# A transformer block on one Trainium2 core: weights between block products and heads split sooner, the second sums of x on GpSimd, the gates of the first head one product sooner

## The chip, the cores and the metric

One core of a Trainium2 chip runs the whole kernel in one launch. The metric is the time of one execution on the device in microseconds; the kernel before took 791.63 us (median of 3 runs, 791.51 to 792.37).

Names in the profile: PE is TensorE (PEld its weight loads), DVE is VectorE, ACT is ScalarE, POOL is GpSimd, SP is SyncE, which issues most of the DMAs. L93 is line 93 of the kernel that the profile belongs to. All line numbers in the text up to the prediction are those of the kernel before.

## The reference

A block with 512 tokens and a model width of 1024: a norm, one wide input projection, a gated linear attention (GLA) with 4 heads in two directions, a latent attention (MLA) with 8 heads, a merge of the two by gates, an output projection, and an MLP with a squared ReLU. Cut to what matters here:

```python
proj = rmsnorm(h, g_mix) @ w_in
(gq, gk, gv, gr, z_gf, z_gb, cq, ckv, kr, z_ma, z_mb) = split(proj)
# GLA, for each of 4 heads, forward and backward, in chunks:
la = log_sigmoid(z_g @ w_gate + b_gate) / 16
b = cumsum(la)                       # the decays
scores = (q * exp(b)) @ (k * exp(-b)).T, masked
y_gla = rmsnorm(scores @ v + state part) * silu(gr)
# MLA from the latents cq (384 wide) and ckv (256 wide), with rotary parts
merged = sigmoid(z_ma) * y_gla + sigmoid(z_mb) * y_mla
h = h + merged @ w_out
h = h + square(relu(rmsnorm(h) @ w_ff1)) @ w_ff2
return rmsnorm(h, g_final)
```

Everything is float32 and has to be computed to nearly that precision.

## The kernel before

**Three matmuls for one.** A float32 operand is split into a high part that TensorE takes as it is (`fp32r`) and the rest, the low part. A product is then high x high, high x low and low x high (`mm3`, L88 to L90). `split` (L92) makes the two: ScalarE copies the high half (L93), VectorE subtracts it from the source (L94). A product can't start before the high half of its weights is there, nor go beyond its second matmul before the low half is.

**Weights.** `weights` (L218) takes a staging tile `wf` (3 buffers), loads it by a DMA from SP's queue, takes tiles for the halves (`wh`, `wl`, 4 buffers each) and splits. `proj_begin` (L231) does that for 128 columns of `w_in` and takes a PSUM bank; `proj_run` (L235) issues the 24 matmuls of 128x512. A 512 KB load waits until its staging buffer's last reader is done, so the loads run about three projections ahead.

**The order of work.** Instructions are traced in the order of the Python code. A scheduler then sets each engine's order, except where `in_program_order` chains the instructions of an engine as they were traced, and `goes_behind` puts one stretch behind another. Each engine then works through its own queue in order; an instruction that waits holds up all behind it.

**The stretch that is edited** runs from the projections' beginning to the end of the GLA heads:

1. `x_sums` (L533): from the transposed input `xraw`, GpSimd makes sums `xy` (two per pair of blocks, L541 and L542), which are split into `xsy`. `more_x_sums` (L551) makes the sums `xz` on VectorE (L556, L557) and splits them into `xsz`.
2. Two block products, `gr` and `gv` (class `Seven`, L563), each a 512x1024x1024 product done as a Strassen-like scheme of seven half-size products, in the order 1, 2, 5, 6, 3, 7, 4. `prepare(m)` subtracts blocks of weights in place on VectorE (L580) and splits them; `product(m)` runs 24 matmuls of 128x512 onto two PSUM banks and evicts: products 1, 5 and 6 by a ScalarE copy (L627), products 2, 3 and 7 by a VectorE addition in place (L632) and then a sink, product 4 by the sink alone. Products 1, 6, 7 and 4 add onto the same two banks (`grx`, `gvx`), products 5 and 3 onto two others (`grz`, `gvz`). The sink of `gr` (`gr_rows`) is a tanh and a product (L640, L641), that of `gv` (`gv_rows`) a scaled split (L97, L98).
3. Between these products stand other projections, the `fillers`: `zb4` behind product 2 of `gr`, `z_chunk` (the weights `wz`, for gates and rotary keys) behind its product 7, `gq1` behind product 2 of `gv`. A loop (from L934) prepares two products ahead.
4. `gates_begin(h)`: two matmuls of the gates of head h, abs, exp and log on ScalarE (L413 to L418), a minimum on VectorE (L415). `gates_end(h)`: for each direction (`decays`) four scans on VectorE (L431), a difference (L435), three exponentials on ScalarE (L439, L440, L446), small copies on GpSimd. `gla_qk`: four products on VectorE (L460) and scaled copies on GpSimd (L468).
5. The heads loop: scores of head h, gates of head h+1, projections `za`, `gq`, `gk`, the product with v (`gla_out`), the row squares, the gated rows (L689), and `gla_turn`, which transposes them (`y`, L699). In the last round `ckv0`, `ckv1` and `cq0` (class `Latent`) stand where `gq` and `gk` stood.

From `heads_from` to the loop's end ScalarE and VectorE keep the traced order (`SPLITTERS`); TensorE keeps it from the first block product on (`PE_ONLY`); GpSimd keeps it in the stretch of 1 to 3.

Of the kernel before, what the change touches and what calls it, by code (L numbers as in the profile page):

```python
# [14 lines left out]
AF = mybir.ActivationFunctionType  # L15
# [41 lines left out]
def tile_block(ctx: ExitStack, tc: tile.TileContext, t, out: bass.AP):  # L57
# [13 lines left out]
    def u4(name, dt=F32R, shape=(P, 2, S)):  # L71
        return tl(list(shape), dt, "u4", 26, name)
# [4 lines left out]
    def ps(tag, name):  # L77
        serial[0] += 1
        return pp.tile([P, S], F32, tag=tag, bufs=4, name=f"{name}_{serial[0]}")
# [27 lines left out]
    def traced():  # L107
        return len(nc.cur_bb.bb.instructions)
# [15 lines left out]
    def goes_behind(late, early, engines):  # L124

        ins = nc.cur_bb.bb.instructions
        for e in engines:
            a, b = [[i for i in ins[x:y] if i.engine == e] for x, y in (early, late)]
            if a and b:
                issued_after(b[0], a[-1].name)  # L130
# [98 lines left out]
    def proj_begin(w, col, name, tag="mm"):  # L229
        wh, wl = weights(w[:, col : col + P], name)  # L230
        return wh, wl, ps(tag, name)  # L231

    def proj_run(begun, src, half=None, ks=range(KD)):
        wh, wl, acc = begun
        c = slice(0, S) if half is None else slice(half * 256, half * 256 + 256)  # L235
        for k in ks:
            mm3(acc[:, c], wh[:, k, :], wl[:, k, :], src[k][:, 0, c], src[k][:, 1, c], k == 0, k == KD - 1)
        return acc
# [106 lines left out]
    def gated(acc, name):  # L345

        z = u2(f"z{name}")
        nc.vector.tensor_tensor(z, acc, R, op=ALU.mult)
        th = u2(f"t{name}")
        nc.scalar.activation(th, z, AF.Tanh, scale=0.5)  # L350
        return z, th

    def qk_normed(h, x, acc):
        n = u2(f"{'gq' if x == 0 else 'gk'}n{h}")
        if x == 0:
            nc.vector.scalar_tensor_tensor(n, acc, GQ_SCALE, R, op0=ALU.mult, op1=ALU.mult)
        else:
            nc.vector.tensor_tensor(n, acc, R, op=ALU.mult)
        return n
# [15 lines left out]
                gates[d][64:128, :], wg_raw[d][64:128, :], raw(gates[d][64:128, :]), op=ALU.subtract  # L375
            )

    def z_chunk(tag):
        wf = stage(KD, 64, "wz")
        w3 = w_in.rearrange("(k p) w -> p k w", p=P)  # L380
        nc.sync.dma_start(wf[:, :, 0:32], w3[:, :, C_ZG : C_ZG + 32])
        nc.sync.dma_start(wf[:, :, 32:64], w3[:, :, C_KR : C_KR + 32])

        w, _ = halves(KD, P, "wz")
        split(w[:, :, 0:64], w[:, :, 64:128], wf)
        acc = ps(tag, "zk")
        for k in range(KD):
            for x in range(2):
                nc.tensor.matmul(
                    acc, w[:, k, :], xT[k][:, x, :], start=k == 0 and x == 0, stop=k == KD - 1 and x == 1  # L390
                )
        both = u2("zkl")
        nc.scalar.activation(both[0:64, :], acc[64:128, :], AF.Copy)
        nc.vector.tensor_tensor(both[0:64, :], acc[0:64, :], both[0:64, :], op=ALU.add)
        nc.vector.tensor_tensor(kr[0:64, :], both[0:64, :], R[0:64, :], op=ALU.mult)
        nc.scalar.activation(z4[0:32, :], kr[0:32, :], AF.Copy)
        nc.vector.tensor_tensor(z4[32:64, :], kr[0:32, :], raw(z4[0:32, :]), op=ALU.subtract)
        nc.vector.tensor_copy(z4[64:128, :], raw(z4[0:64, :]))
        for a, b in ((32, 48), (48, 32)):
            nc.sync.dma_start(kswap[a + 32 : a + 48, :], kr[b : b + HALF, :])  # L400
            nc.sync.dma_start(kr[a + 32 : a + 48, :], kr[a : a + HALF, :])
# [19 lines left out]
    def gates_end(begun):  # L421
        l, ms = begun
        return {d: decays(d, l[:, i], ms[i]) for i, d in enumerate(("f", "b"))}
# [25 lines left out]
    def project_qk(h, x):  # L449
        col, name = ((C_GQ, "gq"), (C_GK, "gk"))[x]  # L450
        qk[h, x] = qk_normed(h, x, proj_T(col + h * P, f"{name}{h}"))
# [81 lines left out]
    def x_sums():  # L533

        add = nc.gpsimd.tensor_tensor
        for p in range(KD // 2):
# [10 lines left out]
            x_left.append({m: (src[:, 0, c], src[:, 1, c]) for m, src, c in (  # L547
                (1, upper, LO), (2, lower, LO), (4, lower, HI), (5, sy, LO), (6, sy, HI),
            )})

    def more_x_sums():  # L551
        add = nc.vector.tensor_tensor
        for p in range(KD // 2):
            a, b = xraw[p], xraw[p + KD // 2]
            z = u2(f"xz{p}")
            add(z[:, LO], a[:, LO], a[:, HI], op=ALU.subtract)  # L556
            add(z[:, HI], b[:, LO], x_y[p][:, HI], op=ALU.subtract)  # L557
            sz = u4(f"xsz{p}")
            split(sz[:, 0], sz[:, 1], z)
            x_left[p][7] = sz[:, 0, LO], sz[:, 1, LO]  # L560
            x_left[p][3] = sz[:, 0, HI], sz[:, 1, HI]
# [147 lines left out]
    class Latent:  # L709
        def __init__(self, col, n, gcol, name):  # L710
            self.col, self.n, self.gcol, self.name = col, n, gcol, name
            self.cs, self.sqs = [], []

        def begin(self, j):
            self.begun = proj_begin(w_in, self.col + j * P, f"{self.name}{j}")

        def run(self, j):
            acc = proj_run(self.begun, xT)
            c = u2(f"{self.name}c{j}")
            nc.scalar.activation(c, acc, AF.Copy, scale=gvec[:, self.gcol + j : self.gcol + j + 1])  # L720
            s = u2(f"{self.name}s{j}")
            nc.scalar.activation(s, acc, AF.Square)
            if self.sqs:
                nc.vector.tensor_tensor(s, s, self.sqs[-1], op=ALU.add)
            self.cs.append(c)
            self.sqs.append(s)
# [187 lines left out]
    def zb_gate(f, tag="mm"):  # L914
        g2.append(gated(proj_T(C_ZB + f * P, f"zb{f}", tag), f"b{f}")[1])
# [7 lines left out]
    for x in (0, 2, 1, 3):  # L923
        sevens[0].load(x)
    loading = loading, traced()
    fillers = {
        (0, 2): lambda: zb_gate(4), (0, 7): lambda: z_chunk("mm"),
        (1, 2): lambda: project_qk(1, 0),
    }
    steps = [(a, m) for a in range(2) for m in SEVEN]  # L930
    ordered = traced()
    for a, m in steps[:2]:
        sevens[a].prepare(m)
    for n, (a, m) in enumerate(steps[:-2]):  # L934
        ahead = steps[n + 2]
        filled = (a, m) in fillers
        if a == 0:
            for x in {3: (0,), 7: (2, 1), 4: (3,)}.get(m, ()):
                sevens[1].load(x)
        if filled:  # L940
            sevens[a].product(m)
            at = traced()
            fillers[a, m]()
            goes_behind((at, traced()), loading, (mybir.EngineType.SP,))
        sevens[ahead[0]].prepare(ahead[1])
        if n == 2:
            more_x_sums()
        if (a, m) == (0, 5):
            load_gates()
            pos_i = u2("pos_i", I32)  # L950
            nc.gpsimd.dma_start(pos_i, t["positions"][0].partition_broadcast(P))
        if (a, m) == (0, 4):
            split_gates()
        if not filled:
            sevens[a].product(m)
# [1 line left out]

    def begin(col, name):  # L960
        return proj_begin(w_in, col, name)

    def begin_za(f):
        return begin(C_ZA + f * P, f"za{f}")

    def begin_qk(h, x):
        col, name = ((C_GQ, "gq"), (C_GK, "gk"))[x]
        return begin(col + h * P, f"{name}{h}")

    heads_from = traced()  # L970
    gated_now = gates_begin(0)
    w_k = begin_qk(1, 1)
    parts = gates_end(gated_now)
    sevens[1].product(7)
    near, nxt, far = gla_qk(0, parts)
    w_b = begin(C_ZB + 5 * P, "zb5")
    qk[1, 1] = qk_normed(1, 1, proj_run(w_k, xT))
    sevens[1].product(4)
    w_a = begin_za(0)
    g2.append(gated(proj_run(w_b, xT), "b5")[1])  # L980
    ckv_, cq_ = Latent(C_CKV, 2, V_KV, "ckv"), Latent(C_CQ, 3, V_Q, "cq")
    for h in range(GH - 1):
        sc = gla_scores(near, nxt, far)
        gated_now = gates_begin(h + 1)
        w_b = begin_za(2 * h + 1)
        acc = proj_run(w_a, xT)
        parts = gates_end(gated_now)
        za_gate(2 * h, acc)
        os = gla_out(h, sc)
        near, nxt, far = gla_qk(h + 1, parts)  # L990
        if h < 2:
            w_a = begin_qk(h + 2, 0)
        else:
            ckv_.begin(0)
        rs = gla_squares(h, os)
        za_gate(2 * h + 1, proj_run(w_b, xT))
        if h < 2:
            w_b = begin_qk(h + 2, 1)
            gla_gated(h, os, rs)
            qk[h + 2, 0] = qk_normed(h + 2, 0, proj_run(w_a, xT))  # L1000
            w_a = begin_za(2 * h + 2)
            qk[h + 2, 1] = qk_normed(h + 2, 1, proj_run(w_b, xT))
        else:
            ckv_.run(0)
            ckv_.begin(1)
            gla_gated(h, os, rs)
            ckv_.run(1)
            cq_.begin(0)
        gla_turn(h)
    in_program_order(heads_from, SPLITTERS)  # L1010
    in_program_order(ordered, PE_ONLY)
# [411 lines left out]
```

## Time and profile before

| what | value |
|---|---|
| median of 3 runs | 791.63 us |
| the profiled execution, whole | 793.04 us |
| its span, first to last instruction | 791.3 us |
| TensorE busy | 765.2 us, 97% |
| VectorE busy | 572.5 us, 72% |
| ScalarE busy | 442.7 us, 56% |
| GpSimd busy | 107.5 us, 14% |
| block product `gr` on TensorE, with its fillers | from 40.62 to 91.27 us |
| block product `gv`, with its fillers and the first gates | from 91.27 to 146.87 us |
| first scores of head 0 | 153.40 us |
| `cq0`, last projection of the heads loop | from 264.64 us |

The profile comes from one execution. Matmuls are pipelined and their ends are modelled, so 97% says that TensorE rarely waits, not that it works at its peak. A busy share is a mean over the whole span; a single stretch has its own limit.

In a timeline a line reads: start in us from the span's start, duration, engine, line, operation, tile written <- tiles read, partitions x elements, count, and in brackets how long the engine was idle before and which instruction ended it. In the list of waits a line reads: engine, tile and line that waited, then what it waited for, and us in total, times, longest.

### The profile page before, as it was taken

Reading aid. Unit: us, or ns where it says so; the run is one execution under the profiler, and the core shown is the slowest. Engines: PE = TensorE matmul, PEld = TensorE weight load, DVE = VectorE, ACT = ScalarE, POOL = GpSimd, SP = SyncE. Lnnn points to the kernel's source line nnn. Section 1 sums busy time; section 2 is a strip of 40 time slices with the busy share of each in tenths; the row PEclk is TensorE's granted clock in tenths of the full one; section 3 lists DMA queues with packets and bytes.
Section 4 is the critical chain, followed back from the end, with each engine's and each line's share of the span. In section 5 each row is a group of like instructions: output and inputs, shape, how many; then the busy total and the mean of one; then the engine's idle time right before and its main releaser. Section 6 shows DMA issues by size and latency. Waiting matters only on the chain.

```text
span 791.3 us, 10153 instructions
## 1 busy us (share of the span) xinstructions
PE 765.2 (97%) x3768; PEld 641.6 (81%) x3768; DVE 572.5 (72%) x858; ACT 442.7 (56%) x749; POOL 107.5 (14%) x182
## 2 busy tenths in 40 slices
PE   9999998899998999999999999999999999999996
PEld 7777876778786788888988898888888888888885
DVE  7799986665556667599993478875788487857695
ACT  7556547473745455698872366544653456436644
POOL 0400000442606002321120000000000000000014
PEclk9999999999999999999999999999999999999999
DMA  9617111212212433322114642064105501450002
GB/s 324 221 43 222 35 27 27 55 28 80 54 53 57 133 48 75 90 75 60 54 41 152 215 153 70 16 208 138 48 27 180 166 27 53 157 169 23 27 1 106
DMA packets 93185, 73.94 MB, mean 93 GB/s; under 512 B 15088, under 2 KB 74480, under 8 KB 93136
## 3 DMA queue, kind: packets, MB, share of 16 engines
q1 hardware_dynamic: 92048, 70.14, 30.1%
q10 hardware_dynamic: 864, 2.38, 0.8%
q0 software_dynamic: 224, 0.79, 0.4%
q8 instruction: 29, 0.48, 0.3%
q14 instruction: 20, 0.16, 0.1%
HBM read 69.62 MB, written 2.10 MB: 91 GB/s over the span
## 4 chain that ended last, share of the span: by engine, by line
PE 79%; DVE 11%; ACT 8%; issue 2%; POOL 1%; DMA 0%; SPq 0%; POOLq 0%; DVEq 0%; ACTq 0%
PE f L89 7%; PE f L90 7%; PE f L88 7%; PE gx L88 4%; PE gx L89 4%; PE gx L90 4%; PE first L311 2%; PE wo L88 2%; PE wo L89 2%; PE gz L89 2%; PE wo L90 2%; PE gz L90 2%; PE gz L88 2%; PE tp L891 2%; PE zb L90 1%
## 5 line engine op out<-in xcount | busy, mean ns | idle before, releaser
L1362 POOL DMA_DIRECT2D gfin<-in_g_final x1 | 0.7, 653 | 282.6 <-PE f L90 282.6
L1187 DVE TENSOR_TENSOR w<-w,w 128x1024 f32<-128x1024 f32 x32 | 38.7, 1220 | 0.4
L874 DVE TENSOR_REDUCE top<-s 128x1 f32<-128x512 f32 x32 | 21.7, 679 | 5.2 <-PE s L90 5.1
L877 ACT ACTIVATE e<-s,top 128x512 f32<-128x512 f32 x32 | 21.9, 686 | 5.6 <-DVE top L874 2.9
L1134 DVE TENSOR_TENSOR h<-gx,h 128x512 f32<-128x512 f32 x32 | 21.5, 683 | 1.8 <-PE gx L90 1.7
L94 DVE TENSOR_TENSOR pT<-tp,pT 128x512 fp32r<-128x512 f32 x32 | 21.6, 678 | 0.8 <-ACT pT L93 0.7
L442 POOL COPY v3f<-rrf 128x4 f32<-128x4 f32 x4 | 2.8, 709 | 138.2 <-DVE rrf L431 138.2
L93 ACT ACTIVATE pT<-tp 128x512 fp32r<-128x512 f32 x32 | 19.0, 595 | 4.0 <-PE tp L891 3.8
L891 PE MATMUL tp<-ident,e 128*128 128x128 f32 x128 | 19.2, 272 | 0.0
L88 PE MATMUL av<-pT,v 128*128 128x256 f32 x64 | 19.1, 298 | 0.0
L909 POOL TENSOR_TENSOR tb<-tb,za 128x512 f32<-128x512 f32 x8 | 11.2, 1402 | 54.8 <-DVE tb L908 40.4
L1240 ACT ACTIVATE fa<-f 128x512 f32<-128x512 f32 x32 | 18.5, 578 | 0.0
L89 PE MATMUL av<-pT,v 128*128 128x256 f32 x64 | 18.5, 288 | 0.0
L891 PEld LDWEIGHTS tp<-ident,e 128*128 128x128 f32 x128 | 15.4, 140 | 3.5 <-PE s L90 0.6
L90 PE MATMUL av<-pT,v 128*128 128x256 f32 x64 | 18.2, 285 | 0.0
L93 ACT ACTIVATE gbh<-y 128x512 fp32r<-128x512 f32 x16 | 10.1, 634 | 14.0 <-DVE y L1257 14.0
L94 DVE TENSOR_TENSOR sc<-sc,sc 128x512 fp32r<-128x512 f32 x16 | 10.9, 690 | 9.5 <-ACT sc L93 9.5
L93 ACT ACTIVATE sc<-sc 128x512 fp32r<-128x512 f32 x16 | 9.3, 596 | 11.5 <-DVE sc L517 11.5
L88 PE MATMUL s<-kbuf,q 96*128 96x512 f32 x32 | 14.0, 438 | 1.2 <-DVE grb L689 0.9
L93 ACT ACTIVATE b_10h<-w 128x1024 fp32r<-128x1024 f32 x7 | 7.4, 1059 | 12.1 <-PE gx L90 6.0
L93 ACT ACTIVATE b_20h<-w 128x1024 fp32r<-128x1024 f32 x7 | 7.4, 1059 | 12.1 <-PE gx L90 6.0
L93 ACT ACTIVATE b_00h<-w 128x1024 fp32r<-128x1024 f32 x7 | 7.4, 1057 | 12.0 <-PE gx L90 6.0
(1569 smaller groups left out, 2884.0 us busy)
## 6 DMA issues: line engine op xcount, KB each, us to landing
w<-in_w_ff SPq DMA_DIRECT2D x64, 256.0 KB, 3.4
grw<-in_w_in SPq DMA_DIRECT2D x8, 512.0 KB, 7.8
gvw<-in_w_in SPq DMA_DIRECT2D x8, 512.0 KB, 4.8
x<-in_xt SPq DMA_DIRECT2D x8, 256.0 KB, 5.4
vw<-in_w_first SPq DMA_DIRECT2D x8, 256.0 KB, 5.4
h<-in_x ACTq DMA_DIRECT2D x4, 512.0 KB, 5.2
out<-ms SPq DMA_DIRECT2D x7, 256.0 KB, 2.2
q<-ro SPq DMA_DIRECT2D x16, 64.0 KB, 2.3
```

Of the source, the lines that this page charges most:

```text
L88: nc.tensor.matmul(acc, lh, rh, start=start, stop=False, skip_group_check=onto)
L89: nc.tensor.matmul(acc, lh, rl, start=False, stop=False, skip_group_check=onto)
L90: nc.tensor.matmul(acc, ll, rh, start=False, stop=stop, skip_group_check=onto)
L93: nc.scalar.activation(hi, src, AF.Copy)
L94: rest.tensor_tensor(lo, src, raw(hi), op=ALU.subtract)
L311: nc.tensor.matmul(f_accs[i], a[:, i * P : (i + 1) * P], b, start=k == 0 and x == 0, stop=k == KD - 1 and x == 2)
L874: nc.vector.tensor_reduce(top, acc, axis=AX.X, op=ALU.max, negate=True)
L877: nc.scalar.activation(e, acc, AF.Exp, bias=top, accum_out=tot)
L891: nc.tensor.transpose(tp[:, k * P : (k + 1) * P], e[:, k * P : (k + 1) * P], ident)
L1134: nc.vector.tensor_tensor(hc, acc, hc, op=ALU.add)
L1187: nc.vector.tensor_tensor(wq[dst][g], wq[x][g], wq[y][g], op=op)
L1240: nc.scalar.activation(a, acc, AF.Relu)
```

## The change

The four parts of the diff:

- **Fillers.** Each filler is now a pair: a first part that loads and splits the weights, traced ahead of the block product, and a rest with the matmuls, traced behind it. `z_chunk` is cut into `z_chunk_begin` and `z_chunk_run` for that.
- **Sums of x.** The two operations for each `xz` move from `more_x_sums` on VectorE into `x_sums` on GpSimd. `more_x_sums` only splits them, and is traced ahead of the next `prepare`.
- **First gates.** The loop over products ends one earlier. The gates of head 0 are begun, product 4's weights of `gv` prepared, `gk1` begun and the decays traced ahead of products 3 and 7 of `gv`; before, only product 7 stood behind them. `zb5` is begun ahead of `gla_qk(0)`.
- **Heads.** `begin_late` loads the weights and makes the high half; the low half is a closure, called between the decays of the two directions. `gq2`, `gq3` and `ckv0` use it. `ckv0` runs behind the gated rows, and `cq0` begins ahead of `ckv1`'s run. `Latent` keeps the begun projections by number for that.

```diff
+    def begin_late(col, name):
+
+        wf = stage(KD, P, name)
+        nc.sync.dma_start(wf, w_in[:, col : col + P].rearrange("(k p) w -> p k w", p=P))
+        wh, wl = halves(KD, P, name)
+        nc.scalar.activation(wh, wf, AF.Copy)
+
+        def lows():
+            nc.vector.tensor_tensor(wl, wf, raw(wh), op=ALU.subtract)
+
+        return (wh, wl, ps("mm", name)), lows
...
-    def z_chunk(tag):
+    def z_chunk_begin(tag):
...
-        acc = ps(tag, "zk")
+        return w, ps(tag, "zk")
+
+    def z_chunk_run(begun):
+        w, acc = begun
...
-
-    def more_x_sums():
-        add = nc.vector.tensor_tensor
         for p in range(KD // 2):
             a, b = xraw[p], xraw[p + KD // 2]
             z = u2(f"xz{p}")
             add(z[:, LO], a[:, LO], a[:, HI], op=ALU.subtract)
             add(z[:, HI], b[:, LO], x_y[p][:, HI], op=ALU.subtract)
+            x_z.append(z)
+
+    x_z = []
+
+    def more_x_sums():
+        for p, z in enumerate(x_z):
             sz = u4(f"xsz{p}")
             split(sz[:, 0], sz[:, 1], z)
...
     fillers = {
-        (0, 2): lambda: zb_gate(4), (0, 7): lambda: z_chunk("mm"),
-        (1, 2): lambda: project_qk(1, 0),
+        (0, 2): (lambda: begin(C_ZB + 4 * P, "zb4"), lambda w: finish_zb(4, w)),
+        (0, 7): (lambda: z_chunk_begin("mm"), z_chunk_run),
+        (1, 2): (lambda: begin_qk(1, 0), lambda w: finish_qk(1, 0, w)),
     }
...
-    for n, (a, m) in enumerate(steps[:-2]):
+    for n, (a, m) in enumerate(steps[:-3]):
...
         if filled:
+            first_part, rest = fillers[a, m]
+            at = traced()
+            w = first_part()
+            goes_behind((at, traced()), loading, (mybir.EngineType.SP,))
             sevens[a].product(m)
-            at = traced()
-            fillers[a, m]()
-            goes_behind((at, traced()), loading, (mybir.EngineType.SP,))
-        sevens[ahead[0]].prepare(ahead[1])
+            rest(w)
         if n == 2:
             more_x_sums()
+        sevens[ahead[0]].prepare(ahead[1])
...
     heads_from = traced()
     gated_now = gates_begin(0)
+    sevens[1].prepare(4)
     w_k = begin_qk(1, 1)
     parts = gates_end(gated_now)
+    sevens[1].product(3)
     sevens[1].product(7)
+    w_b = begin(C_ZB + 5 * P, "zb5")
     near, nxt, far = gla_qk(0, parts)
-    w_b = begin(C_ZB + 5 * P, "zb5")
-    qk[1, 1] = qk_normed(1, 1, proj_run(w_k, xT))
+    finish_qk(1, 1, w_k)
     sevens[1].product(4)
...
         acc = proj_run(w_a, xT)
-        parts = gates_end(gated_now)
+        if h < 2:
+            w_a, lows = begin_late(C_GQ + (h + 2) * P, f"gq{h + 2}")
+        else:
+            ckv_.begun[0], lows = begin_late(C_CKV, "ckv0")
+        l, ms = gated_now
+        parts = {"f": decays("f", l[:, 0], ms[0])}
+        lows()
+        parts["b"] = decays("b", l[:, 1], ms[1])
         za_gate(2 * h, acc)
         os = gla_out(h, sc)
         near, nxt, far = gla_qk(h + 1, parts)
-        if h < 2:
-            w_a = begin_qk(h + 2, 0)
-        else:
-            ckv_.begin(0)
...
         else:
-            ckv_.run(0)
             ckv_.begin(1)
             gla_gated(h, os, rs)
+            ckv_.run(0)
+            cq_.begin(0)
             ckv_.run(1)
-            cq_.begin(0)
         gla_turn(h)
```

The order that the scheduler makes of it: TensorE's order differs in one place alone, the two gate matmuls of head 0, which stand ahead of product 3 of `gv` instead of behind it. On ScalarE the four splits of `xz` stand around the splits of product 5's weights of `gr` and ahead of that of `zb4`; the splits of `gq2`, `gq3` and `ckv0` ahead of the table load for the exponentials; `ckv1`'s ahead of the copies of `ckv0`'s result. On VectorE the subtraction for `zb4` stands ahead of the second of two evictions instead of behind it, and that for `gq1` where it stood. On SP two loads for `gv` stand further forward, and `zb5`'s ahead of the small copies of the rotary keys. GpSimd has eight operations more, directly behind the `xy` sums, and in the heads the small copies of the second direction behind those of the first.

## The prediction

> **What bounds the kernel now.** I read the page first, then the list of who waited for whom on TensorE, then the timeline of each engine around each of those waits.
>
> ```profile
> span 791.3 us, 10153 instructions
> PE 765.2 (97%) x3768; PEld 641.6 (81%) x3768; DVE 572.5 (72%) x858; ACT 442.7 (56%) x749; POOL 107.5 (14%) x182
> ```
> TensorE is busy for 97% of the span, and its chain sets the end. The change adds and removes no matmul, so it can only gain what TensorE idles. The waits on TensorE in the stretch that is edited (engine, tile, line waited for: us, times, longest):
>
> ```profile
> PE ckv L88 <- ACT ckv1h L93: 2.2, 1, 2.2
> PE gk L88 <- ACT gk1h L93: 2.1, 1, 2.1
> PE zb L90 <- DVE zb4l L94: 1.6, 1, 1.6
> ...
> PE gvx L88 <- DVE gvc L632: 1.4, 1, 1.4
> PE cq L88 <- ACT cq0h L93: 1.3, 1, 1.3
> PE gq L90 <- DVE gq1l L94: 1.0, 1, 1.0
> ...
> PE zb L90 <- DVE zb5l L94: 0.8, 1, 0.8
> PE grz L88 <- ACT grc L627: 0.7, 1, 0.7
> ```
> Nearly all are weights of a projection that were split (ScalarE the high half, L93, VectorE the low half, L94) too late. TensorE starts a 128x512 matmul every 0.227 us when nothing is late; I size a wait by what the distance of two starts in its timeline has over that, which is 0.05 to 0.2 more than this list says, and add 0.11, by which the first interval after a wait was longer.
>
> One wait cost more than itself. Stretch, then sum of busy us and count for PE, PEld, DVE, ACT, POOL, then the granted clock:
>
> ```profile
> 251.98:255.45 3.47, 0.89 (x3) 0.30 (x2) 1.12 (x1) 2.12 (x3) 0.32 (x2) 1.00 0.00 0
> 255.45:258.86 3.41, 3.25 (x8) 2.58 (x9) 2.49 (x7) 0.00 (x0) 0.00 (x0) 0.50 0.60 154
> 262.27:265.68 3.41, 1.77 (x11) 1.09 (x9) 2.00 (x3) 3.21 (x5) 0.00 (x0) 1.00 0.00 0
> ```
> After 3.4 us with 0.9 busy (the waits for ckv1h and ckv1l) the granted clock was 0.50 for 3.41 us and eight matmuls started 0.43 apart: 1.6 us lost. After 1.77 busy it stayed at 1.00.
>
> **The change part by part.** Times are of the execution before; each part is worked out as if TensorE came to it when it did there, and the shifts are added. The order on each engine is that of the two built programs.
>
> *x sums on GpSimd: +2.3, then -0.9.* Eight 128x256 operations (8 x 0.42 us on VectorE) now stand on GpSimd behind the xy sums, which end at 33.05. What the two engines do to each other there:
>
> ```profile
> 28.96 1.59 POOL L542 TENSOR_TENSOR xy<-xy,x 128x256 f32<-128x256 f32 x1
> 30.52 1.72 POOL L541 TENSOR_TENSOR xy<-x,x 128x256 f32<-128x256 f32 x1
> 32.31 0.74 POOL L542 TENSOR_TENSOR xy<-xy,x 128x256 f32<-128x256 f32 x1
> 28.19 1.77 DVE L94 TENSOR_TENSOR zb2l<-zb2f,zb2h 128x1024 fp32r<-128x1024 f32 x1
> 31.56 0.68 DVE L356 SCALAR_TENSOR_TENSOR gqn<-first,R 128x512 f32<-128x512 f32 x1
> 35.25 2.50 DVE L94 TENSOR_TENSOR xsy<-xy,xsy 128x512 fp32r<-128x512 f32 x4 [1.22 <-ACT xsy L93]
> ```
> zb2l, with both inputs in SBUF, took 1.77 beside GpSimd against 1.22 alone, and the xy operations 1.6 to 1.7 against 0.74; gqn, which reads PSUM, kept its 0.68. So each such VectorE operation waits out one of GpSimd's and the reverse. GpSimd's eight (0.72 apart, three free ones until 35.25) now run beside the four xsy low halves, so these take turns at 1.17 (two 128x512 operations on the diagonal, 25.19 and 26.36, were that far apart beside GpSimd) and not at 0.60: they end at 39.95 and not at 37.66, +2.3. Queued behind them on VectorE is zb2's product with R, behind that on ScalarE its tanh, behind that gr10h. TensorE's first product then starts its second matmul at 43.55 and not at 41.27: **+2.3**. Bounds: 0, if GpSimd were done before the low halves, and 3.9, if the wait also slows the clock (1.6, above). I take 2.3, since both engines' start times are rows. What is gained: the split of the sums is out of the way at 70, where grc, late behind xsz, held product 3 of the gr weights for **0.85**. The 2.7 us that VectorE saves are otherwise no gain: it idles soon after.
>
> *zb4: 0.* zb4h moves up in the source, but on ScalarE the four xsz halves (0.55 each) now stand before it: gra 46.18 to 47.37, one xsz, gr50h, gr51h (0.95 each), three xsz, so zb4h runs 51.45 to 52.5 and not at 49.63. On VectorE one xsz low half (0.6) is added before gr50l, one sum of gra (0.6) moves behind zb4l: zb4l starts at 53.0, before at 53.08. The wait of 1.79 stays. *gq1: 0*: its place in both queues is what it was (behind a subtraction of gvw that ends at 102.5). Of its 1.13 and of zb4's 1.79 nothing is expected; both bounds are below.
>
> *Gates of head 0 before product 3: -0.4, and +1.3 of clock.* The two gate matmuls go from 125.22 to 119.78. ScalarE's abs, exp and log follow gvb's copies at 121.55 and end 4.6 later at 126.2; gv40h and gv41h (0.96 each) now stand behind them; then gk1h, which needs a buffer that product 7 frees half way (125.67 + 12 x 0.227 = 128.4, plus 0.25, as gv40h followed): 128.65 and not 132.28. gk1l comes at 129.73 and not at 133.35, 3.6 earlier, in time for gk1 at 131.1: its waits (2.26 + 0.70 + 0.22 = 3.2) go. But the evictions of products 3 and 7 are now both queued behind the decays on VectorE, one after the other, and product 4 of the gv weights adds onto the banks that the last two read. A round of them:
>
> ```profile
> 141.20 0.69 DVE L632 TENSOR_TENSOR gvc<-gvx,gvc 128x512 f32<-128x512 f32 x1
> 141.92 0.72 ACT L97 ACTIVATE gv<-gvc,r_x 128x512 fp32r<-128x512 f32 x1 [1.42 <-DVE gvc L632]
> 142.68 0.75 DVE L98 SCALAR_TENSOR_TENSOR gv<-gvc,r_x,gv 128x512 fp32r<-128x512 f32 x1 [0.79 <-ACT gv L97]
> ```
> 2.14 until VectorE's next operation at 143.34 (2.69 for the first, which waits for the exponentials). There were two rounds from 138.51; now four from 134.89: the third sum ends at 140.4, the fourth at 142.55. TensorE is through gk1 at 136.55, waits 3.9, does three matmuls, waits 1.4, and goes on at 142.6 where it went on at 141.94: the 3.2 are given back and **+0.66** with them. zb5l now precedes the qk products and ends at 145.6, before it is wanted: its 0.95 + 0.11 go. Sum **-0.4**. The idle stretch is longer than the one before the row of 0.50, so I add **+1.3** for the clock (0 to 1.6: part of the slow 3.4 us can fall into the wait). The Trainium skill ("TensorE: Matmul & The Clock Gate", section "What's actually happening") has the clock halved after a whole idle window of about 3.4 us. The row at 251.98 was slowed with 0.9 us of work in it, so it is the row that I follow; by the rule the 3.9 us would hold a whole window only at a lucky phase, and the sum would be 1.3 lower.
>
> *Heads: -11.3.* The first split of each head's product (gq2, gq3, ckv0) moves between the two directions of the decays. On ScalarE gq2h (0.95) falls into 2.0 us in which eef waits for diff: free. On VectorE gq2l (1.14) makes the second direction and all behind it 1.14 later (rrb 169.85 to 171.0, the exponentials of b, za's product, the qk products); gq2h leaves the queue behind them, so gk2h comes at 178.65 and not at 178.90, and gk2l ends at 181.05. gq2 now starts at 174.9 without a wait (0.74 + 0.70 + 0.22 = 1.66 gone), so gk2 wants gk2l at 180.8: 0.35 comes back. **-1.3**; the same at gq3 (0.63 + 0.78 + 0.22 - 0.35 = **1.3**) and ckv0 (0.63 + 0.79 + 0.22 = **1.6**). GpSimd's chain also starts 1.14 later, but one of its operations no longer meets gq2l (1.62 against 0.57), so it ends at 181.7 as before, and the gated rows are ready at 185.1 for y, which TensorE now wants at 186.2: covered by 1.1. ckv1h no longer stands behind the two copies of ckv0's result: 248.5 and not 253.24. Gone are 2.37 + 0.70 + 0.22 and the 1.6 of slow clock, less 0.3 for ckv1l: **-4.6**. cq0h and cq0l no longer wait for ckv1's copies: cq0l ends at 256.2, wanted at 257.3; 1.55 + 0.69 + 0.22 = **-2.5**. DMAs: gq2f, gq3f and ckv0f were issued 18 us or more before their new splits; two gvw loads pass wzf, gq1f and gk1f on SP's queue, 0.5 us each, where those have tens of us.
>
> Sum: 2.3 - 0.85 - 0.4 + 1.3 - 11.3 = **-9.0**. The profiled execution took 793.0 (span 791.3, 1.7 around it), so 784.1; the median of the runs is 1.4 lower, 791.6, so **782.7**.
>
> **The rivals.**
> - The clock stays full at product 4: -1.3, 781.4. For it: 1.65 us idle in a window left it at 1.00. Against it: 3.9 is far more. 0.10.
> - The clock is slowed after the first wait as well (2.3 idle between 40.8 and 43.55, one matmul in it): +1.6, 784.3. 0.15.
> - GpSimd's sums are hidden (the 2.3 does not come): 780.4. Against it the row of 1.77. 0.10.
> - zb4 and gq1 are split early after all: -1.79 - 1.13 - 0.22, 779.6. Against it the queues. 0.04.
> - The heads' waits move on to gk2, gk3 and ckv1: the low half behind them comes later by what the product came earlier, 1.3 + 1.3 + 1.6 back: 786.9. For it the 0.35 already there. 0.10.
> - Slower: GpSimd holds each head's gated rows. Its eight qk operations took 0.57 alone and 1.6 beside VectorE; two of eight met it before. If more meet it now that they start 1.14 later, each costs 1.0, and y waits from the second on (cover 1.1). Over three heads, four more give back 8.7, the whole gain; all seven free ones 17.7: 800. Against it: VectorE is idle for 2 us or more in that stretch. 0.11, of it 0.03 within 0.2%.
>
> **How the numbers follow.** The forecast has 0.40. The range: 778.9 (port hidden and clock full) to 789.0 (moved waits and one more slow window); outside are the slower rival and little else. Less than 0.2% (1.6 us) can't be told from no change here. Faster 0.89, same 0.03, slower 0.08.
>
> **What would show it.** In the profile of the changed kernel: xsy low halves 1.2 apart and the first grx later against zb3's end; zb4l and gq1l still in the list of waits; no wait for gk1h, but one of some 3.9 and 1.4 for gvc and a granted clock of 0.5 behind it; no waits for gq2, gq3, ckv0, ckv1h, cq0, short ones for gk2l, gk3l, ckv1l; no slow clock near 256. Wrong it is if y waits for the gated rows, or product 4 starts right behind gk1.

## The result and the profile after

The changed kernel took 784.82 us (median of four runs: 783.95, 784.01, 785.63, 785.91) against 791.59 for the kernel before beside it, a ratio of 0.9913 (95% interval 0.9896 to 0.993): faster by 0.9%. The forecast was 782.7, range 778.9 to 789.0. The profiled execution took 784.01, 9.03 below the profiled one of before; the sum of terms said 9.0.

The first lines of the page of after, and its list of who waited for whom on TensorE (engine, tile, line waited for: us, times, longest):

```profile
span 782.3 us, 10154 instructions
PE 763.6 (98%) x3768; PEld 642.4 (82%) x3768; DVE 571.2 (73%) x850; ACT 443.8 (57%) x749; POOL 113.4 (14%) x190
```

```profile
PE gvx L88 <- DVE gvc L650: 4.4, 2, 3.7
...
PE grx L88 <- ACT gr10h L93: 1.3, 1, 1.3
PE zb L90 <- DVE zb4l L94: 1.1, 1, 1.1
PE gq L90 <- DVE gq1l L94: 1.0, 1, 1.0
...
PE grx L89 <- DVE gr10l L94: 0.8, 1, 0.8
...
PE zb L88 <- ACT zb4h L93: 0.2, 1, 0.2
```

The waits for gk1, zb5, grc, gq2, gq3, ckv0, ckv1 and cq0 are gone. gq1l stands where it stood; zb4l is down from 1.6 to 1.1, with 0.2 new at zb4h. New are gr10h and gr10l at the first product, and gvc has grown from 1.4 to 4.4 at product 4 of `gv`. The eight operations more on POOL and fewer on DVE are the x sums; here they are, from the timelines of GpSimd and of VectorE (start us, us, engine, line, operation):

```profile
34.34 0.74 POOL L568 TENSOR_TENSOR xz<-x 128x256 f32<-128x256 f32 x1
...
36.88 1.18 POOL L569 TENSOR_TENSOR xz<-x,xy 128x256 f32<-128x256 f32 x1
38.02 1.18 POOL L568 TENSOR_TENSOR xz<-x 128x256 f32<-128x256 f32 x1
```

```profile
35.19 4.56 DVE L94 TENSOR_TENSOR xsy<-xy,xsy 128x512 fp32r<-128x512 f32 x4 [1.23 <-ACT xsy L93]
39.67 0.68 DVE L360 TENSOR_TENSOR zb<-zb,R 128x512 f32<-128x512 f32 x1
42.00 1.23 DVE L94 TENSOR_TENSOR gr10l<-grw,gr10h 128x1024 fp32r<-128x1024 f32 x1 [1.65 <-ACT gr10h L93]
...
135.73 0.68 DVE L650 TENSOR_TENSOR gvb<-gvz,gvb 128x512 f32<-128x512 f32 x1
...
138.42 0.68 DVE L650 TENSOR_TENSOR gvb<-gvz,gvb 128x512 f32<-128x512 f32 x1
...
140.56 0.69 DVE L650 TENSOR_TENSOR gvc<-gvx,gvc 128x512 f32<-128x512 f32 x1
...
142.71 0.68 DVE L650 TENSOR_TENSOR gvc<-gvx,gvc 128x512 f32<-128x512 f32 x1
```

The four xsy low halves took 4.56 us where they took 2.50, and an xz operation beside them 1.18 where it takes 0.74 alone: the turns of the prediction. Below stand the four rounds of evictions, 2.69, 2.14 and 2.15 apart; TensorE adds product 4 onto the banks that the last two read. What that does to it (TensorE's timeline, then stretches with sum of busy us and count for PE, PEld, DVE, ACT, POOL and the granted clock):

```profile
137.20 0.39 PE L90 MATMUL gk<-xT,gk1l 128*128 128x512 f32 x1
141.30 0.61 PE L88 MATMUL gvx<-gv40h,xT 128*128 128x512 f32 x1 [3.71 <-DVE gvc L650]
...
143.45 0.80 PE L88 MATMUL gvx<-gv40h,xT 128*128 128x512 f32 x1 [0.68 <-DVE gvc L650]
```

```profile
134.72:138.14 3.42, 2.87 (x13) 2.06 (x11) 2.05 (x5) 2.25 (x6) 2.15 (x12) 1.00 0.11 34
138.14:141.55 3.41, 0.25 (x1) 0.25 (x2) 2.31 (x4) 0.99 (x2) 0.00 (x0) 1.00 0.00 0
141.55:144.96 3.41, 2.73 (x7) 1.62 (x7) 2.10 (x3) 1.99 (x3) 0.00 (x0) 0.50 0.00 0
144.96:148.38 3.42, 3.42 (x10) 2.68 (x9) 3.25 (x4) 0.14 (x1) 1.34 (x2) 0.50 0.19 38
39.16:42.57 3.41, 2.03 (x8) 1.12 (x6) 1.76 (x3) 2.18 (x3) 2.82 (x5) 1.00 0.00 0
```

TensorE stood still for 3.87 us (start to start less 0.227), did three matmuls, stood for 1.09 more, and its clock was 0.50 not for one stretch of 3.41 us but for two. The slow stretch at 255 us of the kernel before is gone.

How much later each tile started on TensorE than before adds it up: second matmul of the first product +2.0; product 3 of `gr` +1.05; product 7 of `gv` +0.88; bd, the first scores, +2.68; ckvss, behind the heads, -9.06, and no change from there to the end.

### The profile page after: what moved, and what is told of

It is laid out like the page before. It is cut to its first block, busy times and chain, and to the rows that moved or that the text cites. A ratio compares the mean times of both kernels' runs of the same rounds, so it can differ in the third digit from the quotient of the medians.

```text
span 782.3 us, 10154 instructions
## 1 busy us (share of the span) xinstructions
PE 763.6 (98%) x3768; PEld 642.4 (82%) x3768; DVE 571.2 (73%) x850; ACT 443.8 (57%) x749; POOL 113.4 (14%) x190
## 4 chain that ended last, share of the span: by engine, by line
PE 89%; DVE 6%; ACT 2%; issue 1%; DMA 1%; POOL 0%; SPq 0%; POOLq 0%; DVEq 0%
PE f L89 8%; PE f L88 7%; PE f L90 7%; PE gx L88 4%; PE gx L89 4%; PE gx L90 4%; PE first L323 2%; PE za L88 2%; PE za L89 2%; PE wo L90 2%; PE wo L89 2%; PE gz L89 2%; PE za L90 2%; PE gz L88 2%; PE gz L90 2%; PE wo L88 2%
```

## The experiments

Times are medians of four to twelve runs. The kernel before, run beside them, had medians of 793.0, 794.5 and 795.0 in the three sittings (791.3 to 795.5 for single runs, at granted clocks that don't sort them). A part of such a spread lies ahead of everything edited: the second projection (`first1`) starts on TensorE anywhere from 10.76 to 11.79 us in the thirteen profiles. What makes the rest is not shown. So an edit is read against the changed kernel (784.82, and 784.98 in the last sitting; it was not run in the other two) and from the traces, and a difference of 1 us stands on the traces alone.

**The changed kernel again.**

> The changed kernel once more, beside the two below. If the two values of its first four runs (784.0 and 785.6 to 785.9) are a slow clock window behind the first product's wait that comes in some executions and not in others, its times fall near these two again, the profile has the window near 43 us or has it not, and they differ by some 1.7. If they were only scatter, nothing lies between the granted clocks of the two.

784.98: 783.61 and 783.81 at a mean clock of 0.994, 784.98, 786.03 and 786.22 at 0.992. The profile, of the 784.98, has a stretch of 0.50 from 43.12 to 46.53 us, right behind the first product's wait, which the profile of the first 784.01 has not. By their mean clocks, five of its nine runs have one slow stretch more than the other four, and that is what lies between its two values, near 784.0 and 785.8.

**The x sums back on VectorE.**

```
     def x_sums():
...
-            z = u2(f"xz{p}")
-            add(z[:, LO], a[:, LO], a[:, HI], op=ALU.subtract)
-            add(z[:, HI], b[:, LO], x_y[p][:, HI], op=ALU.subtract)
-            x_z.append(z)
+            x_z.append((a, b))
...
     def more_x_sums():
-        for p, z in enumerate(x_z):
+        add = nc.vector.tensor_tensor
+        for p, (a, b) in enumerate(x_z):
+            z = u2(f"xz{p}")
+            add(z[:, LO], a[:, LO], a[:, HI], op=ALU.subtract)
+            add(z[:, HI], b[:, LO], x_y[p][:, HI], op=ALU.subtract)
...
+        sevens[ahead[0]].prepare(ahead[1])
         if n == 2:
             more_x_sums()
-        sevens[ahead[0]].prepare(ahead[1])
```

> The changed kernel with the second x sums back on VectorE, at their old place behind the preparing. Theory (GpSimd's sums make the four xsy low halves take turns with them and the first product of gr starts late): the two waits of grx at 40 to 43 us go, TensorE starts the first product 1.9 to 2.3 us earlier, the wait of grz for grc (0.7) comes back, so 1.1 to 1.4 us faster than the changed kernel, 783.5 against 784.8; if the slow clock that some runs may have there goes too, up to 3, 782. Rival (the sums on GpSimd cost nothing, the later start comes from elsewhere): the waits of grx stay, and the time is 0.85 slower, 785.7.

783.07 (782.38 to 783.25); its profile has no slow stretch at 43, and the mean clock of all its runs is that profile's, 0.994. From its waits on TensorE:

```profile
PE zb L90 <- DVE zb4l L94: 1.7, 1, 1.7
...
PE grz L88 <- ACT grc L646: 0.7, 1, 0.7
...
PE grx L89 <- DVE gr10l L94: 0.3, 1, 0.3
```

The first product's waits are down to 0.3 and grc's is back, as the theory has it; the rival (0.85 slower) falls. Against 784.0, the value of the changed kernel without the stretch at 43, it is 0.9 faster, a little less than the theory's 1.1 to 1.4. zb4's waits show one reason: they are 1.85 here, start to start, against 0.34 and 1.24 in the changed kernel, so moving the sums had given zb4 0.3.

**The gates of the first head back behind product 3.**

```
-for n, (a, m) in enumerate(steps[:-3]):
+for n, (a, m) in enumerate(steps[:-2]):
...
-    sevens[1].prepare(4)
...
-    sevens[1].product(3)
     sevens[1].product(7)
-    w_b = begin(C_ZB + 5 * P, "zb5")
     near, nxt, far = gla_qk(0, parts)
+    w_b = begin(C_ZB + 5 * P, "zb5")
```

> The changed kernel with the gates of the first head back behind product 3, and zb5 split behind the qk products. Theory (the four evictions in a row before product 4, 3.9 and 1.1 us of waiting, and two slow clock windows behind them cost more than the waits for gk1 and zb5 that went): the granted clock stays 1.00 around 141 to 148, the waits for gk1h, gvc (1.4) and zb5l come back, and the time is 1.3 us below the changed kernel, 783.5. Rival (the move is a gain of 0.4 or more by itself, and the clock does not matter): 785.2 or more, with TensorE's bd later than in the changed kernel.

783.45. The waits for gk1h (2.1), gvc (1.3) and zb5l (0.8) are back, the clock stays 1.00 from 138 to 148, and against the repeated changed kernel, whose profile has the same slow stretch at 43, bd starts 1.55 us earlier on TensorE, from 0.26 earlier at product 2 of `gr`: 1.3 for this part, with the old waits, as expected. Moving the gates was a loss as long as the evictions stood as they did.

**Seventeen matmuls into the wait.**

```
     finish_qk(1, 1, w_k)
+    for _ in range(17):
+        nc.tensor.matmul(w_b[2], w_k[0][:, 0, :], xT[0][:, 0, :], start=True, stop=True)
     sevens[1].product(4)
```

> The changed kernel with 17 matmuls more on TensorE (128x512, into the bank of zb5, which is begun afterwards and overwrites them) in the 3.9 us in which it waits for the third sum of gvc. Theory (TensorE's slow clock from 141.5 to 148.4 follows from the idle stretch before it): the 17 fit into the wait (17 x 0.227 = 3.86), the granted clock stays 1.00, and the time is 2.4 us below the changed kernel, 782.4, though TensorE has more to do. Rival (the clock is slowed for another reason, or the slow matmuls are hidden by other waits): the clock is 0.5 there still, and the time is the same or up to 0.5 above, 784.8 to 785.3.

782.54 (781.46 to 784.15). The same stretches as above:

```profile
138.14:141.55 3.41, 3.41 (x16) 2.66 (x15) 2.10 (x4) 1.21 (x2) 0.00 (x0) 1.00 0.00 0
141.55:144.96 3.41, 2.24 (x11) 1.50 (x10) 2.15 (x4) 1.91 (x3) 0.00 (x0) 1.00 0.02 5
```

With its wait filled with work of no use, TensorE keeps its clock through the second wait too, and bd starts 2.5 us earlier than in the first profile of the changed kernel (153.56 against 156.08), of which 0.2 is there already at gk1 (131.78 against 131.99). Product 4 starts when it did, less the same 0.2 (141.08 against 141.30). So 2.3 us of the change's loss here is clock alone; the rest is waiting.

**The evictions parted.**

```
     nc.vector.tensor_tensor(c, acc, c, op=ALU.add)
-    self.sink(rb + (2 if m == 7 else 0), int(m != 2), c, c)
+    if late is None:
+        self.sink(rb + (2 if m == 7 else 0), int(m != 2), c, c)
+    else:
+        late.append((rb + (2 if m == 7 else 0), 1, c, c))
...
-    sevens[1].product(3)
-    sevens[1].product(7)
+    late = []
+    sevens[1].product(3, late)
+    sevens[1].product(7, late)
...
     finish_qk(1, 1, w_k)
+    for sunk in late:
+        sevens[1].sink(*sunk)
     sevens[1].product(4)
```

> The changed kernel in which the evictions of products 3 and 7 of gv are parted: the sums that free TensorE's banks stand on VectorE right behind each product, and what is made of them (scaling, high and low half, wanted only by heads 2 and 3) behind gk1's normalization. Theory (product 4 waited only because its banks are read last in four rounds of sum, ScalarE and low half): no wait for gvc, no slow clock, TensorE at product 4 of gv 4 to 5 us earlier and at bd 5 to 7.7 us earlier than the changed kernel, 777.1 to 779.8. Rival (what was queued behind the rounds only takes their place: the qk products on GpSimd are not ready for the scores, or zb5): 2 us at most, 782.8 or more, and a new wait at sc.

777.85 (777.00 to 779.37). The four sums on VectorE are now one behind another:

```profile
137.01 1.28 DVE L650 TENSOR_TENSOR gvb<-gvz,gvb 128x512 f32<-128x512 f32 x2
138.21 1.28 DVE L650 TENSOR_TENSOR gvc<-gvx,gvc 128x512 f32<-128x512 f32 x2
```

No wait for gvc is left and the clock stays full there (the profile's one slow stretch ahead of the end is at 42.83, behind the first product's wait). bd starts 7.1 us earlier than in the repeated changed kernel, which has that stretch too (149.99 against 157.07). Only 0.5 for gk2l is new. So with the evictions no longer going through ScalarE one at a time, head 0's gates ahead of product 3 leave neither the old waits (gk1h, zb5l) nor the new one. What parting the evictions would give with the gates in their old place was not run.

**The splits of gq2, gq3 and ckv0 back; the order of ckv1 and cq0 back; the heads alone.** Three kernels. The first has the old loop but for the new order of `Latent`:

```
-        if h < 2:
-            w_a, lows = begin_late(C_GQ + (h + 2) * P, f"gq{h + 2}")
-        else:
-            ckv_.begun[0], lows = begin_late(C_CKV, "ckv0")
...
+        parts = gates_end(gated_now)
...
         near, nxt, far = gla_qk(h + 1, parts)
+        if h < 2:
+            w_a = begin_qk(h + 2, 0)
+        else:
+            ckv_.begin(0)
```

> The changed kernel with the splits of gq2, gq3 and ckv0 back behind the qk products; the new order of ckv1 and cq0 stays. Theory (these three splits were simply late): the waits for gq2, gq3 and ckv0 come back, and the time is 3.6 to 4.2 us above the changed kernel, 788.4 to 789.0. Rival (the three waits only moved on to gk2, gk3 and ckv1, and all of the gain of the heads is from ckv1 and cq0): 0 to 0.5 above it, 785.

789.38, 4.6 above the changed kernel. The waits are back at gq2 (h and l 0.6 + 0.5), gq3 (0.5 + 0.6) and ckv0 (0.5 + 0.6), none at gk2 or gk3; against the repeated changed kernel they put TensorE back by 1.65 at gk2, 3.07 at gk3 and 4.53 behind ckv. The rival falls.

The second, the other way round:

```
+            ckv_.run(0)
             ckv_.begin(1)
             gla_gated(h, os, rs)
-            ckv_.run(0)
-            cq_.begin(0)
             ckv_.run(1)
+            cq_.begin(0)
```

> The changed kernel with ckv0's product, ckv1's split, ckv1's product and cq0's split in the order of the kernel before; the earlier splits of gq2, gq3 and ckv0 stay. Theory (ckv1h stands behind ScalarE's two copies of ckv0, cq0h behind those of ckv1, and the wait for ckv1 also slows the clock): waits of some 2.2 at ckv1h and 1.3 at cq0h come back, with a window of granted clock 0.5 behind the first, 7.1 us above the changed kernel, 791.9; without the slow window 5.5, 790.3. Rival (ckv1 and cq0 wait for what ckv0's late split made late, and are early once it is early): no wait for ckv1 or cq0, below 786.

793.88, 9.1 above. Its waits:

```profile
PE ckv L88 <- ACT ckv1h L93: 2.2, 1, 2.2
...
PE cq L88 <- ACT cq0h L93: 1.3, 1, 1.3
```

They are those of the kernel before, however early ckv0 is. The clock was 0.50 from 256.16, behind ckv1h, as expected, and also from 266.40, behind cq0h, which it was not before: 1.6 above the 7.1. (The profile is of one of the five runs at a mean clock of 0.986, 794.55 to 795.25; the other seven, at 0.988 or 0.989, took 792.47 to 793.96.) With the first of the two kernels that is 4.5 and 8.9 on TensorE, for 11.7 that the heads gave within the change: the parts add up but for that second slow stretch.

The third is the kernel before with the heads' part alone (its diff is the last two blocks of the change with `begin_late` and `Latent`):

> The kernel before with the part of the heads alone (earlier splits of gq2, gq3 and ckv0, new order of ckv1 and cq0). Theory (the heads give what the prediction put there, and the rest of the change loses): 11.3 to 11.7 us below the kernel before and 2 to 3 below the changed kernel, 780 to 782 where before has 791.6 to 793. Rival (the gain of the heads needs the shifts of the other parts): 9 or less below before, not faster than the changed kernel.

780.99 (780.92 to 781.84), 3.8 below the whole change by the medians; the kernel before beside it had 794.5. TensorE starts ckvss 11.28 us earlier than in the profile of before, where the whole change had 9.06 without the slow stretch at 43. In this profile TensorE is already 0.54 late at bd, ahead of the heads' edit (153.95 against 153.41), so from bd on the heads give 11.8. The rest of the change, then, is a loss: 2.2 at ckvss, 2.7 at bd, and more with that stretch.

**The order of zb4 and gq1 written out.**

```
+            split_at = at, traced()
...
             sevens[a].product(m)
+            all_behind((at, traced()), split_at)
             rest(w)
         if n == 2:
             more_x_sums()
+            all_behind((at, traced()), first_fill)
         sevens[ahead[0]].prepare(ahead[1])
+        if filled and m == 2:
+            first_fill = split_at
+            all_behind((at, traced()), split_at)
+        if n in (2, 3):
+            all_behind((at, traced()), first_fill)
```

`all_behind(late, early)` orders every ScalarE and VectorE instruction of the one stretch behind the last of the other, with no semaphore.

> The changed kernel with an order on ScalarE and VectorE written out where the change only moved the source: zb4's split ahead of the split of the x sums, of product 2's eviction and of the next preparing, and gq1's split ahead of the subtraction of gvw. Theory (the source was moved, but both engines' queues kept the late place): the waits for zb4h, zb4l and gq1l go (0.34 + 1.24 + 1.14), 2.2 to 2.7 us below the changed kernel, 782.1 to 782.6. Rival (what is moved behind is late in its turn, gr60 or gv60 or grw's evictions): 0 to 0.5 below, 784.5, with new waits at product 6 of gr or gv.

782.79 (782.15 to 783.29), though its profile has a slow stretch at 45.24, right behind product 1's wait, and all its runs that profile's mean clock, 0.992: 2.0 below the changed kernel's median, 3.0 below its value with such a stretch (785.8), and 2.6 by the shift on TensorE from the first matmul of zb4 to that of product 5 of `gv`. No wait for zb4 or gq1 is left. The source order had not reached the queues; this does.

**All that helps together.** With the x sums on GpSimd, but later:

```
+        nc.gpsimd.tensor_copy(sm("turn", 1), raw(behind[:, 0, 0:1]))   # behind = gr11l
         for p in range(KD // 2):
...
             z = u2(f"xz{p}")
```

> Late sinks and the written order of zb4 and gq1 together, and the second x sums on GpSimd, but behind a one-element copy of gr11l, so that they begin after the xsy low halves and gr11l (some 45 us). Theory (each wait has its own cause, and the x sums on GpSimd cost only because they ran beside the xsy low halves): 6.7 for the sinks, 2.6 for the order and 2.0 for the x sums below the changed kernel's 784.0, 772.7; no slow clock in the span but at its end, grc's wait stays gone. Rival (GpSimd meets the next splits instead, gr20l and gr21l, and product 2 waits): 774.5 or more with a wait for gr20l or gr21l.

775.32 (774.99 to 776.57): the rival's time, though the wait is not at product 2 but at zb4, and a slow stretch follows it, from 55.75 us in the profile (that of the 776.57), which the theory had ruled out. A view each of its waits, of GpSimd and of VectorE:

```profile
PE zb L90 <- DVE zb4l L94: 2.2, 1, 2.2
```

```profile
43.08 0.74 POOL L572 TENSOR_TENSOR xz<-x 128x256 f32<-128x256 f32 x1
43.78 1.72 POOL L573 TENSOR_TENSOR xz<-x,xy 128x256 f32<-128x256 f32 x1
```

```profile
46.50 3.43 DVE L602 TENSOR_TENSOR grw<-grw,grw 128x1024 f32<-128x1024 f32 x2
49.86 1.76 DVE L94 TENSOR_TENSOR gr50l<-grw,gr50h 128x1024 fp32r<-128x1024 f32 x1
```

Seven of the eight sums take 1.72 against 0.74, and each VectorE operation beside one 1.7 against 1.2; the queue reaches zb4l 2.2 us late.

And with them on VectorE:

> Late sinks and the written order together, and the second x sums back on VectorE. Theory: 6.7, 2.6 and 1.1 below the changed kernel's 784.0, 773.6, with the wait for grc (0.7) back. Rival (VectorE, with the sums back, is late for zb4 or gr60 now that the order is written out): 775 or more.

772.46 (772.39 to 773.20), a ratio of 0.9729 to the kernel before beside it (0.9712 to 0.9746), and 12.5 us below the changed kernel (784.98 in that sitting). No wait for grc either, which the theory had kept; by the list nothing in the edited stretch waits for more than 0.5:

```profile
PE zb L90 <- DVE zb2l L94: 0.5, 1, 0.5
PE gk L90 <- DVE gk2l L94: 0.5, 1, 0.5
PE grx L89 <- DVE gr10l L94: 0.3, 1, 0.3
```

## Why the prediction was right, and where not

**x sums: 2.3 less 0.85.** Right in place and cause. At the first product's second matmul TensorE was 2.0 late, not 2.3, and 0.85 came back at grc. Taking turns was first argued from a few rows; the late sums of the last experiment but one show it on seven more.

**zb4 and gq1: 0.** Right but for 0.2: gq1's gap is 1.14 where it was 1.13; zb4's is 0.34 + 1.24 where it was 1.79. Writing the order out took both away, so it was the queues and not the loads.

**Gates of head 0.** "waits 3.9, does three matmuls, waits 1.4, and goes on at 142.6": it was 3.87, three matmuls, 1.09, and 143.45, which less the 0.88 by which TensorE came later to product 7 is 142.57. That term, -0.4, stands. The clock's, **+1.3, is the one that was mis-sized**: TensorE lost 2.2 from product 7 to bd beyond the other terms (2.68 - 0.88 + 0.4), and 2.3 came back with the wait filled. I had reckoned one slow stretch of 3.41 us, part of it in the wait; there were two.

**Heads: -11.3.** Measured from bd to ckvss, the gain is 11.8 alone and 11.7 within the change. The 0.35 that I took back at gk2l and at gk3l did not come: undoing the early splits cost 4.5 on TensorE where the terms made 4.2. No y waits for the gated rows in the profile after, so the slower rival (GpSimd's qk operations meeting VectorE) did not come about.

**The sum and the median.** That the sum met the profiled execution to 0.03 us is in part luck: its terms were off by 0.9 (the clock, too small), 0.4 (the heads' gain, too small), 0.3 (the x sums, too large) and 0.2 (zb4), and these nearly cancel; and the execution that was profiled happened to be one without a slow stretch at 43. The step from there to the median ("1.4 lower") was wrong. The changed kernel's profiled execution lay 0.8 below its median, because two of its four runs are of the rival "the clock is slowed after the first wait as well" (784.3, to which I gave 0.15; with the repeat it is five of nine). By the runs, that rival and the forecast are two values of one kernel, near 785.8 and 784.0, and the median falls between them. What decides between them stands in the last section.

## What to carry to other kernels

Work moved ahead pays only where every queue it passes lets it through: here the source moved zb4 and gq1 and the engines' queues did not, and a product moved behind gates found its evictions in one line with another's. Part an eviction into what frees the bank and what is made of the result, and put only the first on the path. Price a wait on TensorE with the clock that follows it, and don't put GpSimd beside VectorE where a split is awaited and both work on inputs in SBUF, as here.

## What the runs showed of the hardware

In these profiles the clock goes by a fixed grid. The slow stretches of one execution start a whole number of 3.413 us apart (42.93 and 141.92 in the kernel with the late splits undone: 29 times), and where the grid lies differs from run to run. On that grid, in the ten profiles that have such a stretch ahead of the end, a window in which TensorE at full clock was busy for 1.71 us or less was followed by a slow one, 16 times of 16, and one with 1.76 or more never (busy by the profile, which models the matmuls' ends). The two rows nearest to each other, of the kernel with the written order and of the one with the x sums undone:

```profile
41.82:45.24 3.42, 1.71 (x6) 1.23 (x7) 2.49 (x3) 2.47 (x4) 0.92 (x2) 1.00 0.25 77
```

```profile
134.61:138.02 3.41, 1.76 (x8) 1.13 (x6) 1.93 (x3) 1.98 (x5) 1.46 (x12) 1.00 0.00 0
```

The limit between them is half a window. The Trainium skill ("TensorE: Matmul & The Clock Gate", section "What's actually happening") has the window free-running, which the grid bears out, and the clock halved after an idle one; here half an idle one was enough. At half clock, a window with 2.83 busy or less was followed by another slow one (six of six), one with 3.05 or more by a full one (16 of 16): hence two stretches behind product 4, whose second wait fell into the first of them. It also accounts for the two values of the changed kernel: the 1.50 and 1.03 us in which TensorE stands still around the first product's first matmul fall into one window or are parted by its edge. In the first profile the row at 39.16 above has 2.03 busy, and the clock stayed full; in the repeat the window at 39.71 has 1.34 busy, and the slow stretch followed. The other seven runs have no profile.
